# Other places for the high and low parts of streamed weights in four stages of a two-block transformer kernel

## The chip, the cores and the metric

The kernel runs on one core of one Trainium2 chip. The metric is the time of one execution in device microseconds (us); where there are several runs, the median.

## The reference

Two blocks follow each other on 256 tokens of width 2048, all in fp32. Cut to what the changed stages compute:

```python
# end of the first block
gate, up = jnp.split(_rms(h, n2) @ w_gu, 2, axis=-1)      # w_gu: 2048 x 11264
h = h + (jax.nn.silu(gate) * up) @ w_dn                   # w_dn: 5632 x 2048
# end of the second block
gu = hn @ w_up[l]                                         # 2048 x 11264
g = _dwconv_centred(gu[..., :D_FF_2], ffn_conv_w[l], ffn_conv_b[l])
u = gu[..., D_FF_2:]
f = (jax.nn.gelu(g, approximate=True) * u) @ w_down[l]    # 5632 x 2048
h = h + _rmsnorm(f, post_ffn_gain[l])
```

Ahead of these come, in the first block, an input projection, a recurrent branch (RWKV), an attention branch and their merge, and in the second a long convolution, another attention and their output projection.

## The kernel before

All products with large weights are streams. A *piece* is eight blocks of 128 x 128 weights, 512 KB in fp32. `weights` (L195) fetches a piece on SyncE's queue into a tile wr, and `split` (L191) makes two parts of it: ScalarE casts it to fp32r (the high part, tile wh, L192), and VectorE subtracts that from the original (the low part, tile wl, L193). The activations are held in two such parts as well. `mm3` (L213) then issues three matmuls per block, all into the same sum:

- L216: weights wh (loaded, stationary), activations' high part (moving)
- L217: weights wl, activations' high part
- L218: weights wh, activations' low part

TensorE thus loads a high part twice for each time that it loads a low one. wr, wh and wl have three buffers each, so that fetching and splitting run ahead of the matmuls. A piece is 24 matmuls of 256 columns in three of the stages here.

The tiles wh and wl have room for more than a piece (`ROOM`, 1152 words of 4 bytes per partition, where a piece has 1024), and the argument `off` says at which word of both tiles the piece begins. Only the place of the weights in SBUF within 256 bytes is set by it; blocks follow each other at 512 bytes, and the moving operand's at 1024, so the place is the same for all blocks of a piece. Let the *difference* be the address of the moving operand minus that of the loaded weights, modulo 256 bytes. wh and wl start at the same address modulo 256 in all their buffers, and the moving tiles at 0 bytes beyond that in w_gu and w_up2, at 192 in w_down.

`stream` (L220) yields the blocks of a weight tensor piece by piece. Its argument `off` gives the place, and pieces whose number is in `away` go 16 words further, modulo 64. In the kernel before, all four stages have difference 64 for all pieces but those in `away`, which have difference 0. Difference 0 is called *level* here.

The four stages, in order of time, with the last one outside `stream`:

- `phase_glu`: w_gu, 176 pieces, moving x2h and x2l; `off` 48, away pieces 2 and 6. 88 sums of 16 blocks each, in the PSUM banks d, a, b, c in turn; after each pair of sums VectorE and ScalarE make one of the 44 blocks of the hidden layer.
- `run`: w_down, 88 pieces, moving hh and hl; `off` 32, away pieces 1, 3 and 7. 16 sums of 44 blocks.
- `phase_conv_glu`: w_up2, 176 pieces, moving x4h and x4l; `off` 48, away pieces 16 and 20. The first twelve pieces feed six sums at once while the activations arrive (`group`), the others one sum at a time.
- `phase_last`: w_down2, 88 pieces in four groups of 22. Here the roles are turned: the activations hh and hl are loaded, and the weights move, 512 columns at a time, 12 matmuls to a piece (L951 to L953). `off` is 0, and the moving weights lie 64 beyond the activations, modulo 256.

TensorE takes its work in program order; nothing else in these stages orders it than the arrival of the pieces.

Of the kernel before, what the change touches and what calls it, by code (L numbers as in the profile page):

```python
# [18 lines left out]
P = 128  # L19
# [12 lines left out]
PIECE = 8  # L32
# [25 lines left out]
def in_order():  # L58

    out = [("wf", 0), ("ad", 0), ("gd", 0), ("gd", 1)]  # L60
    g = 0
    for j in range(9):
        if j < 8:
            out += [("k", j), ("v", j), ("r", j)]
        if j:
            out += [("fk", j - 1), ("fq", j - 1), ("fv", j - 1)]
        for _ in range(GATES_PER_PAIR[j]):
            out.append(("g", g))
            g += 1
    return out + [("g", i) for i in range(g, 32)]  # L70


def layout(names):
# [78 lines left out]
class Builder:  # L152
# [39 lines left out]
        self.nc.scalar.copy(hi, src)  # L192
        self.nc.vector.tensor_tensor(out=lo, in0=src, in1=hi.bitcast(F32), op=ALU.subtract)  # L193

    def weights(self, src, kt, pools=None, size=PIECE, tag="w", off=0, pitch=P):  # L195


        nc = self.nc
        praw, phi, plo = pools or (self.wraw, self.whi, self.wlo)
        w = self.tl(praw, [P, size, P], "wr")  # L200
        if pools:
            wh, wl = (self.tl(p, [P, size, P], tag + q, F32R) for p, q in ((phi, "h"), (plo, "l")))
        else:
            wh, wl = (self.tl(p, [P, ROOM], tag + q, F32R) for p, q in ((phi, "h"), (plo, "l")))
            at = 0 if pitch > P else off
            wh, wl = (x[:, at : at + size * pitch].rearrange("p (k c) -> p k c", k=size) for x in (wh, wl))
            wh, wl = (x[:, :, off - at : off - at + P] for x in (wh, wl))
        with self.tc.high_priority(offset=2000):
            nc.sync.dma_start(out=w[:, :kt], in_=src)
            self.split(w[:, :kt], wh[:, :kt], wl[:, :kt])  # L210
        return wh, wl
# [8 lines left out]
    def stream(self, name, off=0, away=(), pitch=P):  # L220

        w = self.a[name]
        for i in range(w.shape[0]):
            o = off(i) if callable(off) else off
            wh, wl = self.weights(w[i], PIECE, off=(o + 16) % 64 if i in away else o, pitch=pitch)
            for k in range(PIECE):
                yield wh[:, k], wl[:, k]

# [94 lines left out]
    def run(self):  # L325
        nc, tc, a, ctx = self.nc, self.tc, self.a, self.ctx
# [15 lines left out]
        with ExitStack() as right:  # L342
            with ExitStack() as pa:
                self.prw = self.pool(pa, "prw")
                self.phase_x(pa)
                self.phase_heads()
            with ExitStack() as pa:
                ph = ExitStack()
                php = self.pool(ph, "ph", side="right")
                self.h = self.tl(php, [P, KT, S], "h")  # L350
                pm = ExitStack()
                pmp = self.pool(pm, "pm", side="right")
                mh = self.tl(pmp, [P, KT, S], "mh", F32R)
                ml = self.tl(pmp, [P, KT, S], "ml", F32R)
                pf = ExitStack()
                filters = self.filters(pf)
                self.phase_merge(pa, mh, ml, filters)
            with ExitStack() as pb:
                xp = self.pool(pb, "x2")
                xh = self.tl(xp, [P, KT, S], "x2h", F32R)  # L360
                xl = self.tl(xp, [P, KT, S], "x2l", F32R)
                st = self.stream("w_o", 32, (15, 19, 23))
                for i in range(KT):
                    ps = self.bank()
                    self.dense(ps, st, KT, mh, ml, al)
                    self.residual(i, ps, "n2", xh, xl)
                    next(filters, None)
                pf.close()
                pm.close()
                self.rstd(self.R[:, :S], self.total(self.acc), S, 1.0 / D, 1e-6)  # L370
                self.dump("h1", self.h)
                pd = ExitStack()
                hp = self.pool(pd, "hp", side="right")
                hh = self.tl(hp, [P, HT, S], "hh", F32R)
                hl = self.tl(hp, [P, HT, S], "hl", F32R)
                self.phase_glu(xh, xl, hh, hl)
            with ExitStack() as pc:
                xp = self.pool(pc, "x3")
                xh = self.tl(xp, [P, KT, S], "x3h", F32R)
                xl = self.tl(xp, [P, KT, S], "x3l", F32R)  # L380
                st = self.stream("w_down", 32, (1, 3, 7))
                for i in range(KT):
                    ps = self.bank()
                    self.dense(ps, st, HT, hh, hl, al)
                    self.residual(i, ps, "pre", xh, xl)
                    if i % 4 == 3:
                        nc.scalar.dma_start(out=spill[:, i - 3 : i + 1], in_=self.h[:, i - 3 : i + 1])
                pd.close()
                self.dump("h2", self.h)
                ph.close()  # L390
                self.rstd(self.R[:, :S], self.total(self.acc), S, 1.0 / D, 1e-6)
                py = ExitStack()
                yp = self.pool(py, "yp", side="right")
                ys = [self.tl(yp, [P, 8, S], n, F32R) for n in ("yhh", "yhl", "yah2", "yal2")]
                rs = [self.tl(yp, [P, S], n) for n in ("Rh", "Ra")]
                self.phase_mix(xh, xl, ys, rs)
            with ExitStack() as pe:
                xp = self.pool(pe, "x4")
                xh = self.tl(xp, [P, KT, S], "x4h", F32R)
                xl = self.tl(xp, [P, KT, S], "x4l", F32R)  # L400
                php = self.pool(pe, "ph2")
                self.h = self.tl(php, [P, KT, S], "h")
                nc.scalar.dma_start(out=self.h, in_=spill)
                pf = ExitStack()
                bring, mix = self.phase_out(pf, ys, rs, xh, xl)
                py.close()
                pd = ExitStack()
                hp = self.pool(pd, "hp2", side="right")
                hh = self.tl(hp, [P, HT, S], "hh2", F32R)
                hl = self.tl(hp, [P, HT, S], "hl2", F32R)  # L410
                self.phase_conv_glu(xh, xl, hh, hl, bring, mix, spill2, pf)
                self.dump("h3", self.h)
            with ExitStack() as pg:
                self.phase_last(pg, hh, hl, spill2)
            pd.close()
# [145 lines left out]
    def phase_glu(self, xh, xl, hh, hl):  # L561
        nc, a = self.nc, self.a
        al = slice(0, S)
        R = self.R[:, :S]
        with ExitStack() as c:
            w2 = self.pool(c, "pglu", 2)
            st = self.stream("w_gu", 48, (2, 6))
            for i in range(HT):
                ps = self.bank()
                self.dense(ps, st, KT, xh, xl, al)  # L570
                g = self.tl(w2, [P, S], "glu_g")
                nc.vector.tensor_tensor(out=g, in0=ps, in1=R, op=ALU.mult)
                nc.scalar.activation(out=g, in_=g, func=AF.Silu)
                ps = self.bank()
                self.dense(ps, st, KT, xh, xl, al)
                u = self.tl(w2, [P, S], "glu_u")
                nc.vector.tensor_tensor(out=u, in0=ps, in1=R, op=ALU.mult)
                nc.vector.tensor_tensor(out=u, in0=u, in1=g, op=ALU.mult)
                self.split(u, hh[:, i], hl[:, i])
# [306 lines left out]
    def phase_conv_glu(self, xh, xl, hh, hl, bring, mix, spill, pf):  # L886
# [1 line left out]
        al = slice(0, S)  # L888
        R = self.R[:, :S]
        with ExitStack() as c:  # L890
            st = self.stream("w_up2", 48, (16, 20))
            first = [self.ps(t)[:, :S] for t in "ddaabb"]
            self.nbank = 2
            self.group(first, st, KT, xh, xl, [al] * 6, bring)
# [26 lines left out]
    def phase_last(self, pg, hh, hl, spill):  # L921
# [20 lines left out]
        for g in range(4):  # L942
            gs = slice(512 * g, 512 * g + 512)
            ps = [self.ps("a"), self.ps("d")]
            for i in range(HT // 2):
                wh, wl = (x.rearrange("p (k x) c -> p k (x c)", k=2) for x in self.weights(a["w_down2"][22 * g + i], PIECE))
                for q in range(2):
                    k = 2 * i + q
                    for b in range(2):
                        bs = slice(P * b, P * b + P)  # L950
                        nc.tensor.matmul(ps[b], lhsT=hh[:, k, bs], rhs=wh[:, q], start=k == 0, stop=False)  # L951
                        nc.tensor.matmul(ps[b], lhsT=hh[:, k, bs], rhs=wl[:, q], start=False, stop=False)  # L952
                        nc.tensor.matmul(ps[b], lhsT=hl[:, k, bs], rhs=wh[:, q], start=False, stop=k == HT - 1)  # L953
                if g == 1 and i % 2 and i < 16:
                    turn(i // 2)
# [470 lines left out]
```

## Time and profile before

| what | value |
|---|---|
| median of two runs | 2842.23 us (2840.09 and 2844.37) |
| profiled execution, its own time | 2837.21 us |
| its span, first to last instruction | 2835.2 us |
| mean granted TensorE clock | 0.995 |
| TensorE matmuls, share of the span | 99%, 23288 instructions |
| w_gu, 1012.90 to 1493.05 us of the span | 480.15 us |
| w_down, 1493.05 to 1733.20 | 240.15 us |
| w_up2, 2095.40 to 2578.40 | 483.00 us |
| w_down2, 2578.40 to 2823.40 | 245.00 us |

Times in the profile are of this one execution. PE is TensorE's matmuls, PEld its weight loads, DVE VectorE, ACT ScalarE, POOL GpSimd, SP SyncE. L217 is line 217 of the kernel. A row of the windows view gives a stretch of the span, its length, for each engine the busy time and the number of instructions that ran in it at any time, the granted clock, and the share and rate of DMA. A row of the timeline gives start, duration, engine, line, operation, output <- inputs, and shape. A matmul's record lasts longer than the distance to the next one's start, since matmuls are pipelined; it is the distance, or *spacing*, that adds up to time.

### The profile page before, as it was taken

What the parts mean: (1) busy time and instruction counts of PE and PEld (TensorE: products, weight loads), DVE (VectorE), ACT (ScalarE), POOL (GpSimd) and SP (SyncE); (2) the same over time, 40 slices, a digit from 0 to 9 for tenths busy, and PEclk for the clock granted to TensorE, in tenths of its full rate; (3) what the DMA queues carried; (4) which work ended last, traced back from release to release, by engine and by line L of the source; (5) the groups of instructions that cost most, each with busy time, mean ns of one, the idle gap of its engine ahead of it and who ended that gap; (6) DMA issues with size and microseconds to landing.
All of it is one profiled execution on the core that took longest, in us unless ns stands there. A gap on an engine that the chain in (4) does not pass through costs nothing.

```text
span 2835.2 us, 56206 instructions
## 1 busy us (share of the span) xinstructions
PE 2799.7 (99%) x23288; PEld 2637.9 (93%) x23288; DVE 1849.9 (65%) x2953; ACT 1339.1 (47%) x1986; POOL 171.3 (6%) x325
## 2 busy tenths in 40 slices
PE   8999999999999999999999999999999999999998
PEld 7988888888989999999999999999999999998886
DVE  8857677776567665656565556677787777775444
ACT  6544555555444454444444445544454444444443
POOL 4000000001000200000000000001110000000000
PEclk9999999999999999999999999999999999999999
DMA  6433333334576555555556666444555655556554
GB/s 209 141 109 112 103 118 109 107 107 131 178 240 214 184 190 194 194 193 194 193 194 201 201 201 222 160 145 148 192 192 195 195 194 193 194 194 228 190 191 163
DMA packets 147616, 497.23 MB, mean 175 GB/s; under 512 B 16224, under 2 KB 30816, under 8 KB 146784
## 3 DMA queue, kind: packets, MB, share of 16 engines
q1 hardware_dynamic: 128448, 458.42, 49.2%
q10 hardware_dynamic: 18272, 33.12, 3.4%
q8 instruction: 182, 2.98, 0.4%
q0 software_dynamic: 640, 2.10, 0.3%
q14 instruction: 74, 0.61, 0.1%
HBM read 478.37 MB, written 15.20 MB: 174 GB/s over the span
## 4 chain that ended last, share of the span: by engine, by line
PE 95%; DVE 2%; DMA 2%; ACT 1%; issue 0%; SPq 0%; POOL 0%; ACTq 0%; DVEq 0%; POOLq 0%
PE psd L218 12%; PE psd L217 12%; PE psd L216 12%; PE psb L216 4%; PE psb L218 4%; PE psb L217 4%; PE psc L217 4%; PE psa L217 4%; PE psa L218 4%; PE psc L216 4%; PE psa L216 4%; PE psc L218 4%; PE psa L952 1%; PE psd L953 1%; PE psa L953 1%; PE psd L952 1%
## 5 line engine op out<-in xcount | busy, mean ns | idle before, releaser
L193 DVE TENSOR_TENSOR wl<-wr,wh 128x1024 fp32r<-128x1024 f32 (+1 forms) x872 | 1066.4, 1223 | 640.0 <-ACT wh L192 638.9
L192 ACT CAST wh<-wr 128x1024 fp32r<-128x1024 f32 (+1 forms) x872 | 909.4, 1043 | 1189.1 <-PE psd L218 354.8
L217 PE MATMUL psd<-xh,wl 128*128 128x256 f32 (+2 forms) x1280 | 368.9, 288 | 0.9 <-DVE wl L193 0.9
L218 PE MATMUL psd<-xl,wh 128*128 128x256 f32 (+2 forms) x1280 | 369.7, 289 | 0.0
L216 PE MATMUL psd<-xh,wh 128*128 128x256 f32 (+2 forms) x1280 | 368.7, 288 | 0.9 <-DVE p L1028 0.7
L216 PEld LDWEIGHTS psd<-xh,wh 128*128 128x128 f32 x1280 | 240.6, 188 | 9.1 <-issue 4.1
L218 PEld LDWEIGHTS psd<-xl,wh 128*128 128x128 f32 x1280 | 240.7, 188 | 7.8 <-issue 3.2
L217 PEld LDWEIGHTS psd<-xh,wl 128*128 128x128 f32 x1280 | 240.7, 188 | 6.3 <-DVE wl L193 1.1
L216 PE MATMUL psd<-x3h,wh 128*128 128x256 f32 x496 | 140.7, 284 | 0.1
L218 PE MATMUL psd<-x3l,wh 128*128 128x256 f32 x496 | 140.7, 284 | 0.0
L217 PE MATMUL psd<-x3h,wl 128*128 128x256 f32 x496 | 138.9, 280 | 0.0
L262 POOL TENSOR_TENSOR acc<-acc,ssq 128x256 f32<-128x256 f32 x42 | 58.7, 1397 | 819.3 <-ACT ssq L264 819.2
L216 PE MATMUL psd<-x4h,wh 128*128 128x256 f32 x368 | 100.7, 277 | 2.8 <-ACT x4h L252 2.8
L217 PE MATMUL psd<-x4h,wl 128*128 128x256 f32 x368 | 101.5, 277 | 0.0
L218 PE MATMUL psd<-x4l,wh 128*128 128x256 f32 x368 | 101.3, 277 | 0.0
L217 PE MATMUL psa<-x4h,wl 128*128 128x256 f32 x352 | 97.2, 277 | 0.2 <-DVE wl L193 0.2
L218 PE MATMUL psa<-x2l,wh 128*128 128x256 f32 x352 | 97.4, 277 | 0.0
L216 PE MATMUL psa<-x2h,wh 128*128 128x256 f32 x352 | 97.4, 277 | 0.0
L218 PE MATMUL psb<-x2l,wh 128*128 128x256 f32 x352 | 97.2, 276 | 0.0
L217 PE MATMUL psb<-x2h,wl 128*128 128x256 f32 x352 | 97.2, 276 | 0.0
L216 PE MATMUL psb<-x2h,wh 128*128 128x256 f32 x352 | 97.2, 276 | 0.0
L218 PE MATMUL psc<-x2l,wh 128*128 128x256 f32 x352 | 97.2, 276 | 0.0
(674 smaller groups left out, 8415.8 us busy)
## 6 DMA issues: line engine op xcount, KB each, us to landing
wr<-w_in_dram SPq DMA_DIRECT2D x230, 512.0 KB, 3.4
wr<-w_gu_dram SPq DMA_DIRECT2D x176, 512.0 KB, 3.4
wr<-w_down_dram SPq DMA_DIRECT2D x176, 512.0 KB, 3.4
wr<-w_up_dram SPq DMA_DIRECT2D x176, 512.0 KB, 3.5
wr<-w_ab_dram SPq DMA_DIRECT2D x32, 512.0 KB, 4.6
wr<-w_o_dram SPq DMA_DIRECT2D x32, 512.0 KB, 3.4
wr<-w_out_dram SPq DMA_DIRECT2D x32, 512.0 KB, 4.3
spill_g<-acc ACTq DMA_DIRECT2D x32, 128.0 KB, 2.9
```

The lines of the kernel that those rows point to most:

```text
L192: self.nc.scalar.copy(hi, src)
L193: self.nc.vector.tensor_tensor(out=lo, in0=src, in1=hi.bitcast(F32), op=ALU.subtract)
L216: nc.tensor.matmul(out, lhsT=wh, rhs=xh, start=start, stop=False)
L217: nc.tensor.matmul(out, lhsT=wl, rhs=xh, start=False, stop=False)
L218: nc.tensor.matmul(out, lhsT=wh, rhs=xl, start=False, stop=stop)
L262: nc.gpsimd.tensor_tensor(out=acc, in0=acc, in1=self.pending[id(acc)], op=ALU.add)
L952: nc.tensor.matmul(ps[b], lhsT=hh[:, k, bs], rhs=wl[:, q], start=False, stop=False)
L953: nc.tensor.matmul(ps[b], lhsT=hl[:, k, bs], rhs=wh[:, q], start=False, stop=k == HT - 1)
```

## The change

A new helper, `places(base, first, length, rels)`, returns for each piece number two words, one for wh and one for wl. `rels` is a list of pairs of differences (high, low). The pieces from `first` on are cut into stretches of `length`; the first piece of each stretch is level in both parts, and the others of the stretch have its pair of differences. The pieces before `first` have the first pair, and the last pair goes on to the end. `weights` takes a place for the low part of its own (`offl`), and `stream` passes both on where `off` gives a pair.

w_gu, w_down and w_up2 go through such stretches in place of one place with a few pieces moved: w_gu through eight with level pieces 3, 25, 47, 69, 91, 113, 135 and 157; w_down through four with level pieces 1, 23, 45 and 67; w_up2 through eight with level pieces 17, 37, 57, 77, 97, 117, 137 and 157. The first pair of each is (64, 64), the place that the kernel before has throughout. In w_down2 each of the four groups lies 16 words further than the one before. Nothing else differs: the same instructions on the same data in the same order.

```diff
+def places(base, first, length, rels):
+
+
+    w = lambda r: (base - r) % 256 // 4
+
+    def at(i):
+        s, q = divmod(max(i - first, 0), length)
+        return (w(0), w(0)) if i >= first and q == 0 else tuple(w(r) for r in rels[min(s, len(rels) - 1)])
+
+    return at
...
-    def weights(self, src, kt, pools=None, size=PIECE, tag="w", off=0, pitch=P):
+    def weights(self, src, kt, pools=None, size=PIECE, tag="w", off=0, pitch=P, offl=None):
...
-            at = 0 if pitch > P else off
-            wh, wl = (x[:, at : at + size * pitch].rearrange("p (k c) -> p k c", k=size) for x in (wh, wl))
-            wh, wl = (x[:, :, off - at : off - at + P] for x in (wh, wl))
+            offs = (off, off if offl is None else offl)
+            at = [0 if pitch > P else o for o in offs]
+            wh, wl = (x[:, b : b + size * pitch].rearrange("p (k c) -> p k c", k=size)[:, :, o - b : o - b + P]
+                      for x, o, b in zip((wh, wl), offs, at))
...
-            wh, wl = self.weights(w[i], PIECE, off=(o + 16) % 64 if i in away else o, pitch=pitch)
+            o, ol = o if isinstance(o, tuple) else ((o + 16) % 64 if i in away else o, None)
+            wh, wl = self.weights(w[i], PIECE, off=o, pitch=pitch, offl=ol)
...
-                st = self.stream("w_down", 32, (1, 3, 7))
+                st = self.stream("w_down", places(192, 1, 22, ((64, 64), (208, 208), (240, 240), (160, 160))))
...
-            st = self.stream("w_gu", 48, (2, 6))
+            st = self.stream("w_gu", places(0, 3, 22, ((64, 64), (48, 48), (80, 80), (56, 56), (64, 192), (64, 0), (0, 64), (72, 72))))
...
-            st = self.stream("w_up2", 48, (16, 20))
+            st = self.stream("w_up2", places(0, 17, 20, ((64, 64), (192, 64), (96, 64), (64, 96), (32, 64), (128, 64), (64, 128), (16, 16))))
...
-                wh, wl = (x.rearrange("p (k x) c -> p k (x c)", k=2) for x in self.weights(a["w_down2"][22 * g + i], PIECE))
+                wh, wl = (x.rearrange("p (k x) c -> p k (x c)", k=2) for x in self.weights(a["w_down2"][22 * g + i], PIECE, off=16 * g))
```

## The prediction

> **What bounds the kernel now.** First the page: who is busy, and the chain.
>
> ```profile
> span 2835.2 us, 56206 instructions
> PE 2799.7 (99%) x23288; PEld 2637.9 (93%) x23288; DVE 1849.9 (65%) x2953; ACT 1339.1 (47%) x1986; POOL 171.3 (6%) x325
> PEclk9999999999999999999999999999999999999999
> PE 95%; DVE 2%; DMA 2%; ACT 1%; issue 0%; SPq 0%; POOL 0%; ACTq 0%; DVEq 0%; POOLq 0%
> L193 DVE TENSOR_TENSOR wl<-wr,wh 128x1024 fp32r<-128x1024 f32 (+1 forms) x872 | 1066.4, 1223 | 640.0 <-ACT wh L192 638.9
> L192 ACT CAST wh<-wr 128x1024 fp32r<-128x1024 f32 (+1 forms) x872 | 909.4, 1043 | 1189.1 <-PE psd L218 354.8
> ```
>
> TensorE has 95% of the chain at a full granted clock. A piece's cast (1.04 us) and subtraction (1.22 us) are far below the 2.7 us for which TensorE uses it. So the time of a stage is its matmuls times their spacing. The windows view gives the four stages:
>
> ```profile
> core 0: us, PE busy (x), PEclk, DMA share, GB/s
> 1012.90:1493.05 480.15, 480.15 (x4228) 1.00 0.59 193
> 1493.05:1733.20 240.15, 240.15 (x2115) 1.00 0.60 200
> 2095.40:2578.40 483.00, 482.74 (x4226) 1.00 0.59 195
> 2578.40:2823.40 245.00, 245.00 (x1089) 1.00 0.57 193
> ```
>
> These are w_gu, w_down, w_up2 and w_down2: 1448 of 2835 us, without a gap to speak of. What is left to change is the spacing, so the next windows cut around the moved pieces (w_gu 2 and 6, w_down 3, w_up2 16 and 20). A count includes two matmuls that began ahead of the window, because a record outlasts the spacing; they are taken off.
>
> ```profile
> 1019.30:1022.17 2.87, 2.87 (x26) 1.00 0.57 188
> 1022.17:1030.65 8.48, 8.48 (x74) 1.00 0.58 186
> 1030.65:1033.51 2.86, 2.86 (x26) 1.00 0.57 183
> 1033.51:1113.51 80.00, 80.00 (x708) 1.00 0.59 193
> 1498.79:1501.50 2.71, 2.71 (x26) 1.00 0.60 200
> 1501.50:1504.38 2.88, 2.88 (x26) 1.00 0.59 182
> 2142.72:2145.60 2.88, 2.88 (x26) 1.00 0.60 183
> 2145.60:2153.90 8.30, 8.30 (x73) 1.00 0.57 194
> 2154.07:2156.94 2.87, 2.87 (x26) 1.00 0.61 183
> 2156.94:2236.94 80.00, 80.00 (x708) 1.00 0.59 192
> 2710.00:2810.00 100.00, 100.00 (x439) 1.00 0.57 192
> ```
>
> Read in pairs, these are the argument. A moved piece lies level with the moving operand (difference 0); all others lie at difference 64. Level, a matmul of 256 columns takes 2.88 / 24 = **120.0 ns**. At 64 there are two lasting states: 8.48 / 72 = **117.8 ns** (I call it free) and 80.00 / 706 = **113.3 ns** (held). The same place gives either, with nothing idle and the clock at 1.00; the state changes only at a level piece or a break. And one level piece may not do: in w_gu and in w_up2 the first leads back into free (8.48 us and 8.30 us at 117.8 ns), the second into held. In w_down2, 512 columns take 100.00 / 437 = 228.8 ns.
>
> The timeline shows which load lies beside which matmul:
>
> ```profile
> 1033.41 0.28 PE L216 MATMUL psd<-x2h,wh 128*128 128x256 f32 x1
> 1033.41 0.19 PEld L217 LDWEIGHTS psd<-x2h,wl 128*128 128x128 f32 x1
> 1033.52 0.28 PE L217 MATMUL psd<-x2h,wl 128*128 128x256 f32 x1
> 1033.53 0.19 PEld L218 LDWEIGHTS psd<-x2l,wh 128*128 128x128 f32 x1
> 1033.64 0.28 PE L218 MATMUL psd<-x2l,wh 128*128 128x256 f32 x1
> 1033.64 0.19 PEld L216 LDWEIGHTS psd<-x2h,wh 128*128 128x128 f32 x1
> ```
>
> Each matmul reads its moving operand while the next weights load. In every three, a high part is loaded twice and a low part once.
>
> **What a page makes of it.** By the Trainium skill, page "SBUF — State Buffer", section "Who interferes with whom", TensorE's two reads (moving operand and weight load) have ports of their own and never wait on anyone; by "TensorE: Matmul & The Clock Gate", section "Back-to-back issue gap", warm matmuls come N / 2.4 + 2.5 ns apart, 109 ns for 256 columns, at any place. By that, the change moves nothing. This trace disagrees: 113.3, 117.8 and 120.0 ns at one clock, told apart by place and history.
>
> **The change part by part.** No instruction, byte or wait is added or taken away: the same loads, casts, subtractions and matmuls, at other words of wh and wl. The cast and subtraction write elsewhere; I put that at nothing, since even in series they take 2.27 us of a piece's 2.72. If that cover went, only the excess over 2.7 us per piece would count. DMA is at about 0.6 in these stages, and goes on landing in wr. So there is one kind of cost: matmuls times a change of spacing.
>
> *Level pieces.* w_gu has 8 (3, 25, ... 157) where 2 were moved, w_down 4 for 3, w_up2 8 for 2: 13 more. 13 x 24 x (120.0 - 113.3) = **2.1 us**.
>
> *The first stretches,* still at (64, 64). In w_gu and w_up2 the level piece comes one piece later than the first moved piece did. That is 24 matmuls, whole threes, of the same free state, so I take it to meet the same alignment and to fail in the same way, with no second until pieces 25 and 37. Then pieces 2 and 6 to 24 of w_gu and 16, 18 and 20 to 36 of w_up2 run free, against a before in which piece 3 of w_gu and 17 and 18 of w_up2 did so already and were not counted: net 36 pieces, 36 x 24 x 4.5 = **3.9 us**. If it holds at once, this is nothing or a small gain. In w_down the first moved piece already led to held (the row at 1498.79), and piece 1 stays the level one: nothing.
>
> *Both parts at another place* ((48,48), (80,80), (56,56), (72,72); 208, 240, 160 in w_down; (16,16)): 21 + 21 + 21 + 18 + 62 + 18 = 161 pieces besides the level ones. The trace shows no 256-column matmul at any of these. Bounds: below, 2.1 us of the next window.
>
> ```profile
> 43.60:55.30 11.70, 11.70 (x96) 1.00 0.55 182
> 2098.00:2099.70 1.70, 1.70 (x10) 0.50 0.75 308
> ```
>
> The second row is at a granted clock of 0.50: 1.70 / 8 = 212 ns, so 106 ns at full clock is the floor. The first is the input projection with 272 columns at difference 192: 11.70 / 94 = 124.5 ns, 117.1 ns per 256 columns. Above, level: 120.0 ns. Of four places or states known, three lie between 117 and 120 and one, reached only through a level piece, at 113.3. I take 117.8 for these: 161 x 24 x 4.5 = **17.4 us** (from -28 us at the floor to +26 us at 120.0).
>
> *One part at 64, the other elsewhere.* I let each load carry its own place: 120.0 elsewhere, 113.3 at 64. High elsewhere ((0,64), (192,64), (96,64), (32,64), (128,64): 97 pieces): (113.3 + 2 x 120.0) / 3 = 117.8 ns, 97 x 24 x 4.5 = **10.5 us**. Low elsewhere ((64,192), (64,0), (64,96), (64,128): 80 pieces): (2 x 113.3 + 120.0) / 3 = 115.5 ns, 80 x 24 x 2.2 = **4.2 us**. Bounds as above: 106 and 120.0 ns.
>
> *w_down2.* Here the weights move. Three of four groups (66 pieces, 792 matmuls) go to other differences. 228.8 ns stands 16.8 over twice the floor; held 256 columns stand 7.3 over it, level ones 14. Between 7 and 28 over twice the floor it is -8 to +9 us. With no row for a sign: **0**.
>
> Sum: 2.1 + 3.9 + 17.4 + 10.5 + 4.2 = 38.1 us. The profiled execution took 2837.2 us (span 2835.2) and would take 2875; the median of the two runs before is 2842.2, 5 us above it, so the forecast is **2880 us**, 1.3% slower.
>
> **The rivals.** *The level pieces hold everything.* If the held state is kept by whatever follows a level piece, all new stretches run at 113.3: 2842.2 + 2.1 to 6.0 = 2844 to 2848 us. For it: a level piece is what ended free in three stages. Against it: level matmuls themselves stay at 120.0 beside held neighbours, so the place does count.
>
> *No place matters.* If something else than the place sets the three spacings, nothing changes: 2842 us. The rows above speak against it: level pieces take 120.0 ns in three stages, wherever they stand. This is what the two pages of the Trainium skill would make of the change.
>
> *Faster: a place at which stream and load meet less often.* Free to held was a step of 4.5 ns in the same place. One more step down is 108.8 ns, above the floor of 106. With that in all 338 new pieces: 8112 x 4.5 = 36.5 us off, 2842.2 + 6.0 - 36.5 = 2812 us. It turns to a gain once the mean of the new places falls below 113.3 - 6.0 / 8.112 = 112.6 ns. No 256-column stretch shows less than 113.3, against it.
>
> *Slower by over 2%: nothing holds, and every place costs at least as level does.* 8112 x 6.7 = 54.4, with 6.0 and up to 9 of w_down2: 2903 to 2912 us; over 120 ns it goes on. It decides once the mean of the new places passes 119.6 ns, where 57 us, 2%, are reached. For it: the level rows are the only steady 256-column rows of another place. Against it: the 117.1 of difference 192, and nine stretches that keep one part at 64.
>
> **How the numbers follow.** Forecast, 2856 to 2899 us: 0.58. Held everywhere, 2843 to 2856: 0.14. No place matters, 2842: 0.02. Faster, below that: 0.07. Slower, above 2899: 0.19. Leaving out the faster cases, the unchanged one and a little of held below, and 0.06 above, the range is 2848 to 2911. Two per cent (2785 and 2899), about what can be told from no change here, is passed downward only with all new places near the floor: 0.01. Upward 0.19, within 0.80.
>
> **What would show it.** In the windows view the four stages should take about 496, 247, 498 and 245 us; w_gu from piece 4 to 24 should run at 117.8 ns, and from piece 25 on the spacing should step at each level piece. Held stretches in (48,48) to (80,80) would show the place to be coarser than I take it; a stretch under 113 ns would bear out the faster rival; a mixed stretch at a spacing not between its two places' would refute the adding of loads by thirds. A cast or subtraction over its present duration, or idle time on TensorE, would mean that something besides the spacing counts.

## The result, and the profile after

The changed kernel takes 2880.1 us (median of two runs, 2876.2 and 2884.1) where the kernel before took 2842.2: a ratio of 1.0137, 95% interval 1.0117 to 1.0157. It is slower, by 1.4%.

The page of the changed kernel shows the same work on the same engines; the cast and the subtraction (now L204 and L205, all lines here are 12 to 14 further down) last what they did:

```profile
span 2882.1 us, 56206 instructions
PE 2848.7 (99%) x23288; PEld 2685.9 (93%) x23288; DVE 1850.1 (64%) x2953; ACT 1338.7 (46%) x1986; POOL 170.5 (6%) x325
L205 DVE TENSOR_TENSOR wl<-wr,wh 128x1024 fp32r<-128x1024 f32 (+1 forms) x872 | 1065.8, 1223 | 666.0 <-ACT wh L204 665.0
L204 ACT CAST wh<-wr 128x1024 fp32r<-128x1024 f32 (+1 forms) x872 | 909.1, 1043 | 1235.2 <-PE psd L231 362.8
```

So all of it is in the spacing of the matmuls. The windows view, first by stage (w_gu, w_down, w_up2, w_down2), to be held against 480.15, 240.15, 483.00 and 245.00 us:

```profile
1017.44:1512.70 495.26, 495.26 (x4228) 1.00 0.58 188
1512.70:1759.75 247.05, 247.05 (x2114) 1.00 0.60 194
2125.30:2623.70 498.40, 498.39 (x4226) 0.99 0.58 189
2623.70:2870.40 246.70, 246.70 (x1090) 1.00 0.57 192
```

That is 15.1, 6.9, 15.4 and 1.7 us more, 39 in all. The span grew by 46.9; the other 8 us lie in stages in which nothing was changed, and a second execution of the same kernel has a span of 2877.4.

Now by stretch. Each window leaves out the level piece, the one behind it and the last of the stretch, and is 19 pieces (456 matmuls) in w_gu, 16 in the last window. The eight of w_gu, in the order (64,64), (48,48), (80,80), (56,56), (64,192), (64,0), (0,64), (72,72):

```profile
1032.27:1085.97 53.70, 53.70 (x459) 1.00 0.56 186
1094.47:1147.66 53.19, 53.19 (x458) 1.00 0.59 188
1156.18:1210.02 53.84, 53.84 (x458) 1.00 0.59 186
1218.55:1271.74 53.19, 53.19 (x458) 1.00 0.59 189
1280.14:1331.81 51.67, 51.67 (x458) 1.00 0.60 194
1340.25:1393.95 53.70, 53.70 (x459) 1.00 0.59 186
1402.49:1456.19 53.70, 53.70 (x459) 1.00 0.58 187
1464.73:1509.95 45.22, 45.22 (x387) 1.00 0.59 187
```

53.70 / 456 is 117.8 ns, 53.19 / 456 is 116.6, 53.84 / 456 is 118.1, and 51.67 / 456 is 113.3: one stretch of eight is held, and it is not (64,64) but (64,192). In w_down the stretches run at 113.3 ns for (64,64), 118.3 for 208 and 240, and 117.3 for 160. In w_up2, windows of 17 pieces (408 matmuls; 16 in the last) for (64,64), (192,64), (96,64), (64,96), (32,64), (128,64), (64,128), (16,16):

```profile
2182.08:2228.31 46.23, 46.23 (x410) 1.00 0.60 196
2236.66:2282.89 46.23, 46.23 (x411) 1.00 0.59 194
2291.32:2339.36 48.04, 48.04 (x410) 1.00 0.56 187
2347.91:2395.95 48.04, 48.04 (x410) 1.00 0.57 187
2404.49:2452.99 48.50, 48.50 (x410) 1.00 0.57 185
2461.61:2510.56 48.95, 48.95 (x410) 1.00 0.56 184
2519.13:2566.27 47.14, 47.14 (x411) 1.00 0.58 190
2574.80:2620.87 46.07, 46.07 (x386) 1.00 0.56 184
```

113.3, 113.3, 117.8, 117.8, 118.9, 120.0, 115.5 and 120.0 ns. And w_down2, the second to the fourth group (19 pieces, 228 matmuls), at differences 128, 192 and 0:

```profile
2693.31:2746.29 52.98, 52.98 (x230) 1.00 0.59 189
2754.69:2807.87 53.18, 53.18 (x229) 1.00 0.57 188
2816.17:2867.84 51.67, 51.67 (x230) 1.00 0.49 163
```

232.4, 233.2 and 226.6 ns, where difference 64 has 228.8: one place that is better than the old one.

### The profile page after: what moved, and what is told of

It is laid out like the page before. It is cut to its first block, busy times and chain, and to the rows that moved or that the text cites. A ratio compares the mean times of both kernels' runs of the same rounds, so it can differ in the third digit from the quotient of the medians.

```text
span 2882.1 us, 56206 instructions
## 1 busy us (share of the span) xinstructions
PE 2848.7 (99%) x23288; PEld 2685.9 (93%) x23288; DVE 1850.1 (64%) x2953; ACT 1338.7 (46%) x1986; POOL 170.5 (6%) x325
## 4 chain that ended last, share of the span: by engine, by line
PE 96%; DMA 1%; DVE 1%; ACT 1%; issue 0%; SPq 0%; POOL 0%; DVEq 0%; ACTq 0%; POOLq 0%
PE psd L231 12%; PE psd L230 12%; PE psd L229 12%; PE psb L229 5%; PE psb L231 5%; PE psa L231 5%; PE psa L230 5%; PE psb L230 5%; PE psa L229 5%; PE psc L230 5%; PE psc L231 4%; PE psc L229 4%; PE psa L966 1%; PE psa L967 1%; PE psa L965 1%; PE psd L966 1%
## 5 line engine op out<-in xcount | busy, mean ns | idle before, releaser
L205 DVE TENSOR_TENSOR wl<-wr,wh 128x1024 fp32r<-128x1024 f32 (+1 forms) x872 | 1065.8, 1223 | 666.0 <-ACT wh L204 665.0
L204 ACT CAST wh<-wr 128x1024 fp32r<-128x1024 f32 (+1 forms) x872 | 909.1, 1043 | 1235.2 <-PE psd L231 362.8
L231 PE MATMUL psd<-x2l,wh 128*128 128x256 f32 x352 | 98.4, 280 | 0.0
```

What stands on the lines that cost most here:

```text
L231: nc.tensor.matmul(out, lhsT=wh, rhs=xl, start=False, stop=stop)
```

## The experiments

Three theories were set against each other. By the **place theory** a pair of places has its own spacing, whatever ran before, and only (64,64) has two. By the **entry theory** the pieces before a stretch decide. By the third, the level pieces and what they set off cost the time.

**again**: the changed kernel once more, no edit.

> The changed kernel once more, one look, to see which spacings come back. If the place alone sets a stretch's spacing (place theory), all 20 stretches come back within 0.3 ns, but for the two at (64,64), which may be 113.3 or 117.8 ns. If what precedes a stretch sets it (entry theory), a stretch comes back as long as all that precedes it in its stage comes back too, and stretches of w_up2, whose start has breaks, may differ, by 2 to 5 ns. Time 2876 to 2890 us either way.

2879.4 us. All 20 stretches and the four groups came back, within 0.1 ns, (64,64) too (117.8 in w_gu, 113.3 in w_down and w_up2). The pattern belongs to the kernel, not to the execution; place and entry are not told apart by this.

**level_only**: all level pieces, but only the old place between them.

```diff
-  places(0, 3, 22, ((64, 64), (48, 48), ... (72, 72)))
+  places(0, 3, 22, ((64, 64),))        # w_down and w_up2 likewise
-  ... PIECE, off=16 * g))
+  ... PIECE))
```

> All level pieces of the change stay, all stretches are at (64,64), and w_down2 has one place. If the other places cost the time (place or entry theory), w_gu runs at 117.8 ns in pieces 4 to 24 and at 113.3 from 26 on, w_down and w_up2 at 113.3 but for perhaps one stretch, and the kernel takes 2844 to 2850 us. If the level pieces and what they set off cost it (rival), it stays at 2875 to 2885 us.

2844.8 us against 2840.2, ratio 1.0012 (1.0001 to 1.0024). Its windows for pieces 4 to 24 of w_gu (504 matmuls), 26 to 175 of w_gu and 18 to 175 of w_up2:

```profile
1024.70:1084.05 59.35, 59.35 (x506) 1.00 0.58 186
1086.93:1495.76 408.83, 408.83 (x3601) 1.00 0.60 194
2155.59:2586.35 430.76, 430.76 (x3793) 1.00 0.60 194
```

59.35 / 504 = 117.8 ns; then 113.6 on the mean of 3600, level pieces included. So level pieces and first stretch cost 4 to 5 us, and the other places the remaining 34: the third theory falls.

**no_level**: the changed kernel's stretches without level pieces.

```diff
-  return (w(0), w(0)) if i >= first and q == 0 else tuple(w(r) for r in rels[...])
+  return tuple(w(r) for r in rels[...])
```

> The change without its level pieces: the same stretches, each entered straight from the one before. Place theory: each stretch keeps its spacing of the changed kernel within 0.3 ns, and the kernel is 3 us faster than it, 2875 to 2879 us. Entry theory: at least five stretches change by over 1 ns; those that were held at 113.3 ns, (64,192) in w_gu, (64,64) in w_down and (64,64) and (192,64) in w_up2, go to about 117.8, 8 us together, and the time is 2880 to 2890 us.

2881.9 us, ratio to the kernel before 1.0134 (1.0103 to 1.0165). Neither theory came out whole. (64,64) in w_down and in w_up2 lost its hold and ran at 117.8 ns; (32,64) moved from 118.9 to 117.8, (16,16) from 120.0 to 117.3. The other 16 stretches, and the groups of w_down2, kept their spacing within 0.6 ns. And what I had expected least: (64,192) in w_gu and (192,64) in w_up2 are held without a level piece (20 and 18 pieces, 480 and 432 matmuls, 113.3 ns), the second entered straight from a free stretch (the middle row: 19 pieces, 456 matmuls, 117.8 ns):

```profile
1282.93:1337.32 54.39, 54.39 (x482) 1.00 0.60 194
2186.81:2240.51 53.70, 53.70 (x458) 1.00 0.57 187
2243.28:2292.23 48.95, 48.95 (x434) 1.00 0.60 193
```

**swap**: the lists of w_gu and w_up2 change sides.

```diff
-  st = self.stream("w_gu", places(0, 3, 22, ((64, 64), (48, 48), ...
+  st = self.stream("w_gu", places(0, 3, 22, ((64, 64), (192, 64), ...   # and w_up2 the other
```

> The lists of places of w_gu and w_up2 change sides; the level pieces stay. Place theory: each pair takes its spacing along: (48,48) and (56,56) 116.7 ns, (80,80) 118.1, (64,192) and (192,64) 113.3, (64,0), (0,64), (72,72) and (96,64) 117.8, (32,64) 118.9, (64,128) 115.5, (128,64) and (16,16) 120.0. Entry theory: pairs that stand behind another pair than before, or at another alignment, show another spacing, in steps of about 2 ns, most of all where 113.3 or 117.8 was seen. Time 2876 to 2890 us either way.

2880.4 us. Thirteen of the fourteen pairs besides (64,64) took their spacing along within 0.3 ns: in w_gu (192,64) at 113.3, (128,64) at 120.0, (64,128) at 115.5; in w_up2 (64,192) at 113.3. One did not: (56,56), 116.7 in w_gu, is at 120.0 here. Its 18 pieces (432 matmuls), behind those of (192,64) (19 pieces, 456):

```profile
1084.85:1136.52 51.67, 51.67 (x458) 1.00 0.61 194
2343.86:2395.68 51.82, 51.82 (x434) 1.00 0.56 183
```

And (64,64) lost its hold in w_down, where nothing was edited, as well as in w_up2: it is at 117.8 ns there, behind the same level pieces as in the changed kernel, where it was held. The same 19 pieces (456 matmuls) of w_down, first in the changed kernel, then in this one:

```profile
1521.20:1572.87 51.67, 51.67 (x459) 1.00 0.63 193
1514.24:1567.95 53.71, 53.71 (x459) 1.00 0.57 186
```

So neither the pair nor the stage's own pieces fix the spacing; up to there the two kernels differ only in what ran before the stage. No pair showed more than two lasting spacings in all the runs here, and most showed one.

**two_levels**: a second level piece in each stretch, four pieces behind the first.

```diff
-  ... if i >= first and q == 0 else ...
+  ... if i >= first and q in (0, 4) else ...
```

> Each stretch of the change has a second level piece, four behind its first. By the alignment reason of the prediction, pieces 4 to 6 of w_gu stay at 117.8 ns and those from 8 to 24 go to 113.3, as in the kernel before. If the first stretch is free for another reason, it stays at 117.8 ns. Place theory: all other stretches keep the changed kernel's spacing within 0.3 ns on both sides of the second level piece. Entry theory: (64,0), (0,64), (72,72) and others at 117.8 drop to 113.3 behind it. The time is 2878 to 2884 us by the first, under 2870 by the second.

2872.6 us, between the two ranges; its four stages sum to the changed kernel's 1487 us, so what it is below that kernel's time lies in stages that neither edit touches. Windows of w_gu: pieces 4 to 6 (72 matmuls) and 8 to 24 (408), then of (72,72) behind its second level piece (13 pieces, 312):

```profile
1021.09:1029.56 8.47, 8.47 (x74) 1.00 0.58 189
1032.44:1078.67 46.23, 46.23 (x410) 1.00 0.60 194
1463.61:1501.04 37.43, 37.43 (x314) 1.00 0.59 184
```

117.6, then 113.3: the first level piece fails and the second holds, as in the kernel before. That is what the prediction's alignment step says, but no run moved the alignment by itself. In w_up2 it went the same way here (117.8, then 113.3). (64,0) and (0,64) stayed at 117.8 on both sides; (72,72) went from 117.8 to 120.0, (32,64) from 118.7 to 117.8, (128,64) from 116.7 to 120.0 (the first figures on the three pieces between the level ones). These have two spacings each, none of them 113.3.

**survey**: other pairs, without level pieces.

```diff
-  w_gu rels ((64, 64), (48, 48), ...)
+  w_gu rels ((192,192), (128,128), (0,128), (128,0), (32,160), (96,224), (160,32), (224,96))
+  w_down rels ((192,64), (64,192), (192,192), (128,128))
+  w_up2 rels ((48,176), (80,208), (56,184), (72,200), (64,176), (64,208), (64,160), (64,224))
-  off=16 * g
+  off=(48, 52, 56, 40)[g]
```

> Other pairs, no level pieces: w_gu (192,192), (128,128), (0,128), (128,0), (32,160), (96,224), (160,32), (224,96); w_down (192,64), (64,192), (192,192), (128,128); w_up2 (48,176), (80,208), (56,184), (72,200), (64,176), (64,208), (64,160), (64,224); w_down2 at differences 0, 16, 32, 240. If high and low 128 bytes apart is what made (64,192) and (192,64) run at 113.3 without a level piece, then the pairs that are 128 apart do so too. If it is the pair 64 and 192 alone, the others lie at 115 to 120 ns. (192,192) is 113.3 or 117.8 like (64,64) if the place counts modulo 128, about 118 otherwise. In w_down2 226.7 ns comes back at 0; the three beside it are unknown, 225 to 234. Time 2865 to 2890 us.

2884.5 us. (The fourth group of w_down2 lay at 224, not at the 240 that the expectation names.) Held at 113.3 ns: (192,192) in w_gu and w_down, (192,64) and (64,192) in w_down. Of the others, (56,184) and (64,160) have 115.6; the rest lie between 117.8 and 121.1. So 128 apart is not what holds. w_down2 has 226.7 again at 0, and 231.7, 233.3 and 233.3 at 16, 32 and 224. Windows of 20 pieces (480 matmuls) of (192,192) and (96,224) in w_gu:

```profile
1028.74:1083.12 54.38, 54.38 (x482) 1.00 0.61 196
1339.52:1397.64 58.12, 58.12 (x482) 1.00 0.56 182
```

113.3 and 121.1 ns: over all the kernels here, no whole piece of 256-column matmuls went below the first, and level is not the dearest place.

**hold** and **hold_high**: no moved pieces, one pair in all streams of whole pieces but the input projection, w_down2 at difference 0.

```diff
-  o, ol = o if isinstance(o, tuple) else ((o + 16) % 64 if i in away else o, None)
+  o, ol = (o, (o + 32) % 64) if pitch == P else (o, None)      # hold: (64,192)
+  o, ol = ((o + 32) % 64, o) if pitch == P else (o, None)      # hold_high: (192,64)
-  stream("w_o", 32, (15, 19, 23)); stream("w_q2"); stream("w_k2"); stream("w_out2", 32, (2, 6))
+  stream("w_o", 32); stream("w_q2", 48); stream("w_k2", 48); stream("w_out2", 32)
+  w_down 32, w_gu 48, w_up2 48, w_down2 off=48
```

> The kernel before with the pair (64,192) in all streams of whole pieces but the input projection, no moved pieces, and w_down2 at difference 0 in all groups. If (64,192) comes to 113.3 ns from any state within a piece, the stages with many breaks are held too: the second block's mixing stage, at 117.8 ns now, saves 5 to 8 us, the others 0.5 to 2 us each, w_down2 2.3 us: 10 to 17 us in all, 0.4 to 0.6% faster than the kernel before. If (64,192) only keeps a state that it was entered with, or a break undoes it, only w_down2 gains: 1 to 3 us. Slower than before only if a state above 113.3 lasts in a long stage.

2862.8 us against 2841.3, ratio 1.0075 (1.0061 to 1.0089): slower, where I had expected a gain. It is the case that the expectation names last. Pieces 2 to 175 of w_gu (4175 matmuls), 1 to 87 of w_down (2087) and 18 to 175 of w_up2 (3791):

```profile
1025.24:1521.59 496.35, 496.35 (x4177) 1.00 0.57 185
1524.56:1772.67 248.11, 248.11 (x2089) 1.00 0.59 191
2185.55:2615.18 429.63, 429.63 (x3793) 1.00 0.61 194
```

118.9, 118.9 and 113.3 ns. (64,192) has two spacings as well, and w_gu and w_down, which have no break (no wait of TensorE) behind their first pieces, stay in the dearer one from end to end.

> The same as the run named hold, with the high part at 192 and the low one at 64. If the two parts need only lie 64 and 192 apart from the moving operand, it goes as there, within 3 us. If the part that is loaded twice in three counts more, its recovery behind breaks differs: w_up2's first pieces and the mixing stage show 117 to 120 ns in place of 113.3.

2828.6 us: all four stages held, from the third piece on and behind each break. Not what either expectation says: the order of the two places counts, and it is the pair with the high part at 192 that needs no help.

**high_rep** and **both192**: the kernel of hold_high in six more executions, and the same with both parts at 192.

```diff
-  o, ol = ((o + 32) % 64, o) if pitch == P else (o, None)
+  o, ol = ((o + 32) % 64,) * 2 if pitch == P else (o, None)    # both192
```

> The run hold_high again (high part at 192, low at 64, no moved pieces, w_down2 at difference 0), now timed. If high at 192 comes to 113.3 ns from any state, the same stages show the same spacing as there, and the kernel is 0.35 to 0.5% faster than the kernel before: 2827 to 2832 us. If that was one lucky entry, as (64,192) showed 118.9 in one stage and 113.3 in another, some stage lies at 117.8 to 118.9 and the time is over 2840.

2824.3 us against 2840.4, ratio 0.9942 (0.9928 to 0.9956): **0.6% faster than the kernel before**, and the best version here. The same three windows:

```profile
1014.43:1487.59 473.16, 473.16 (x4177) 1.00 0.59 194
1490.48:1726.99 236.51, 236.51 (x2089) 1.00 0.61 201
2137.66:2567.29 429.63, 429.63 (x3793) 1.00 0.59 194
```

113.3 ns in all. What it gains in the long stages is small, 2 us and 2.3 of w_down2. Another 4.9 us lie in the second block's mixing stage, which has many breaks. There the tile view of x3h gives duration minimum, median and maximum, first of the kernel before, then of this one:

```profile
L216 PE MATMUL psd<-x3h,wh x496: 276/279/467, 1733.3 to 1990.5; 128*128 128x256 f32 x166
```

```profile
L229 PE MATMUL psd<-x3h,wh x496: 276/276/467, 1727.4 to 1979.7; 128*128 128x256 f32 x166
```

In w_gu of the kernel before, pieces at 117.8 ns have a median duration of 279 ns, and those at 113.3 one of 276; in this stage, too, the pieces without a break went from 117.8 to 113.3. The span of the two rows is 257.2 and 252.3 us. The two traces differ by 13.3 us in all; the 4 us that are left lie ahead of w_gu, where two executions of one kernel (hold_high and high_rep) differ by 4.7, so no cause is given for them.

> The same with both parts at 192. If the high part's place alone decides, because it is loaded twice in three, all stages are at 113.3 ns within a piece, as in hold_high, and the time is the same within 3 us. If it takes high and low 128 bytes apart, w_gu or w_up2 shows 117.8 ns like (64,64) does without level pieces, and the kernel is over 2845 us.

2869.1 us, ratio 1.0101 (1.0084 to 1.0118). w_gu runs at 117.8 ns, w_down at 113.3; w_up2 is at 113.3 until the breaks at pieces 11 and 12 and at 117.8 from then on (rows of w_gu and w_up2, pieces as above):

```profile
1019.13:1510.84 491.71, 491.71 (x4177) 1.00 0.57 187
2166.01:2612.50 446.49, 446.49 (x3793) 1.00 0.56 187
```

So the high part's place alone doesn't decide either: (192,192) has the two spacings of (64,64). Of the four pairs that reach 113.3 ns only (192,64) has settled at nothing else, in eight runs of six kernels.

## Why the prediction was right, point by point

It said 2880 us and 1.3% slower; 2880.1 was measured. That the two agree to 0.1 us is luck: the two runs are 2876.2 and 2884.1, and 7.8 us of the longer span lie outside the four stages. So the forecast has to be judged by its terms. Here is the sum, with each piece's time in the changed kernel's trace less the same piece's in the trace before:

| term | forecast, us | measured, us |
|---|---|---|
| level pieces | 2.1 | 2.7 |
| first stretches | 3.9 | 2.3 |
| both parts elsewhere | 17.4 | 17.5 |
| high part elsewhere | 10.5 | 9.8 |
| low part elsewhere | 4.2 | 5.3 |
| w_down2 | 0 | 1.6 |
| sum | 38.1 | 39.2 |

*What bounds it* held: nothing but spacing changed; the cover over cast and subtraction was never used up. *The forecast of stages* (496, 247, 498, 245) came out as 495.3, 247.1, 498.4 and 246.7.

*Level pieces* run at 119.4 to 120.1 ns, as taken. *The first stretch* came out in w_gu, where the first level piece failed each time; that the alignment is the reason fits level_only and two_levels, but is not shown. It was wrong in w_up2: I carried the alignment of the kernel before over a start that has breaks (waits for the arriving activations), and there the one level piece held. In two_levels, whose w_up2 is the same up to piece 20, it failed, and in swap too. In w_down, put at nothing, it held in the changed kernel and failed in swap with the same pieces. So the alignment within the stage does not settle it; what does is open.

*Both parts elsewhere*: 117.8 was taken for eight pairs that have 116.6 to 120.0. The mean is right, but no row of the trace before had one of these places, so that it fell on 117.8 is in part luck too.

*Adding the loads by thirds* is the step that failed. Of nine mixed pairs (one part at 64, the other elsewhere) three have the spacing that it gives: (0,64), (96,64) and (64,128). (64,0) and (64,96) have 117.8 for 115.5, (32,64) and (128,64) 118.9 and 120.0 for 117.8, and (64,192) and (192,64) are held. The two terms come to 15.1 us for 14.7 only because the misses cancel. A spacing belongs to the pair as a whole and to how it was entered; it is not the mean of a cost for each load by its own place.

*The rivals*: held everywhere, no place matters and faster are refuted by no_level and by the stretches themselves. For the faster one, no pair went below 113.3; in w_down2 alone a better place was found. *Slower by over 2%* needed a mean of 119.6 ns over the new places; their 338 pieces have 117.4. A further rival, put at nothing in *The change part by part*, is that the cast and the subtraction slow the matmuls by writing to the new places. In the changed kernel's trace the threes of matmuls that run beside a cast alone, which writes wh, and those beside a subtraction alone, which writes wl, have the same mean spacing within 0.4 ns in each of the 16 stretches of w_gu and w_up2, in 13 of them within 0.1; that speaks against it.

The rule of the Trainium skill, page "SBUF — State Buffer", section "Who interferes with whom", that TensorE's two reads wait on no one, stands against spacings of 113.3 to 121.1 ns at one clock, by place. What waits there, and for what, no run shows. The formula that the prediction takes from the Trainium skill, page "TensorE: Matmul & The Clock Gate", section "Back-to-back issue gap", is by that section the gap of an isolated matmul, and in a stream of weight loads and matmuls both set the spacing. So the section does not say that these streams run at 109 ns.

## What to carry to other kernels

When TensorE is the bound and its clock is full, measure the spacing of the matmuls by stretch against their columns, and try the loaded weights' place against the moving operand's modulo 256 bytes: it changes no instruction, and here it made the kernel 1.4% slower (the change) or 0.6% faster (high_rep). Look for a place that goes to its best spacing by itself, behind any break; one that has to be brought into its good state, as (64,64) here, can lose it at each gap. And a sum that comes out is no proof of its terms: read each of them in the trace after.

## What the runs showed of the hardware that was not expected

- 256 columns with (high, low) at (192,64) came to 113.3 ns from every state seen; the mirror (64, 192) has 113.3 and 118.9; (64,64) and (192,192) have 113.3 and 117.8. A state can last for a whole stage of 4200 matmuls.
- Moving weights of 512 columns: 226.7 ns at difference 0, 228.9 at 64, 231.7 to 233.3 at 16, 32, 128, 192 and 224. For 256 columns of moving activations, difference 0 has 120.0.
- Why these places do so, and why in such steps, no run here shows.
